# A branch prefetch hint on TensorE ahead of each expert's overflow branch

## The chip, the cores and the metric

The kernel runs on one core of a Trainium2 chip. The metric is device time in microseconds (us) of one execution. A core has five engines that each follow their own instruction stream: TensorE (PE; its weight loads are listed as PEld), VectorE (DVE), ScalarE (ACT), GpSimd (POOL) and SyncE (SP, which here issues the weight loads). Each engine has a sequencer that takes instructions in order, waits, branches and hands work to the engine; a "q" behind an engine's name in the trace (PEq, PEldq) is that sequencer.

## The reference

One layer of a hybrid block for 256 latent and 256 context tokens of width 1024, float32 throughout. Modulated RMSNorm, one input projection, four parallel token mixers (grouped attention, neighbourhood attention, Fourier, convolution), a gated merge, an output projection and a gated residual; then a second modulated RMSNorm and a mixture of 16 experts, of which each token uses two; a last RMSNorm. What matters here is the mixture:

```
gate = sum(one_hot(top_idx) * w)                    # two experts of each token
for e in range(16):
    a, b = split(t @ w_gu[e], 2)                    # 256 x 1024 @ 1024 x 1024
    out = out + gate[:, e] * ((silu(a) * b) @ w_down[e])
x = x + g2 * out
```

How many tokens an expert gets is known only when the router has run.

## The kernel before, in words

The first part (up to about 425 us of the span) computes the mixers and the router. The second part is a Python loop over the 16 experts, unrolled into one straight program. Each expert has room for 64 tokens (CAP) in its first block. Its tokens are gathered by one-hot products (`gather_step`, tiles `gag`), four experts at a time; `up` is the first product (tile `gue`, eight steps of two matmuls over the channels), `turned_hidden` turns its result (`hte`), `down` is the second product (`ye`), `slot_gate` (`gse`), `turned` (`ote`) and `scatter` (`sce`) bring the rows back to their tokens. `up` takes a list `beside`: after step k of the first product TensorE does the small pieces of work of the neighbours that stand in `beside[k]`, among them `turn_hidden` of the expert before in step 3.

An expert with more than 64 tokens needs more blocks. The count of each expert is in `cnt`; `values_load` (L1050) puts it in a register of TensorE, VectorE and ScalarE, and `tc.If(rv > CAP)` (L1076) stands around `overflow`, which does the whole chain again for the next 64 tokens, with two more levels inside it (L1078, L1080). The three levels are emitted for each expert, so each expert has a long piece of TensorE code that most executions jump over. All of the expert loop's matmuls are recorded by one helper and so have line L808 (turns: L811); they keep the order in which the code issues them, but a scheduler chooses where the branch of an expert falls between them. In this run's data two of the 16 experts overflow, those of index 5 and 13.

Expert weights come as 1 MB loads from SP (`load_units`, six for an expert: four for the first product, two for the second) into a ring of 16 buffers, each as soon as its buffer is free.

Of the kernel before, what the change touches and what calls it, by code (L numbers as in the profile page):

```python
# [16 lines left out]
ET = mybir.EngineType  # L17
# [4 lines left out]
S = 256  # L22
# [9 lines left out]
CAP = 64  # L32
KC = 31
EPS = 1e-6
# [3 lines left out]
# columns of the packed table of small operands  # L38
# [13 lines left out]
def mixer_moe(ctx: ExitStack, tc: tile.TileContext, A, out, dbg=None):  # L52
    nc = tc.nc
# [32 lines left out]
    # ---------------------------------------------------------------- constants and small operands  # L86
# [17 lines left out]
    # the gate of the second residual, its halves swapped in the second tile  # L104
    G2 = [cp.tile([P, 512], F32, name=f"G2_{i}") for i in range(2)]

    def rstd_of(dst, ssum, n, cols):
        """dst = (ssum / n + EPS) ** -0.5"""
        G.tensor_scalar(dst, ssum, 1.0 / n, EPS, op0=ALU.mult, op1=ALU.add)  # L109
        G.tensor_tensor(dst, dst, mhalf[:, 0:1].to_broadcast([P, cols]) if cols > 2 else mhalf[:, :cols], op=ALU.pow)  # L110
# [8 lines left out]
    # what the branches alone need  # L119
# [11 lines left out]
    def t4(name, shape, dt=F32):  # L131
        """an area of up to 1152 words"""
        n = int(np.prod(shape[1:]))
        t = bp.tile([P, 1152], dt, tag="t4", bufs=4, name=name)[:, :n]
        return t if len(shape) == 2 else t.rearrange("p (a b) -> p a b", a=shape[1])
# [9 lines left out]
    # ---------------------------------------------------------------- modulation  # L145
# [10 lines left out]
    def mod_set(s, out):  # L156
        """one third of the modulation, in steps; [p, j, b, r]: the value of column 512 j + 128 b + p, row r"""
# [19 lines left out]
    def mod_sums(i, res):  # L177
        """part i (of six) of the modulation, for the latent tokens only, without its bias: res gets [p, column],
        still to be summed over the partitions"""
# [16 lines left out]
    def mod_cols(i, dst):  # L196
        """the same as columns: dst [p, b] is its column 128 b + p"""
# [8 lines left out]
    # ---------------------------------------------------------------- norm1 of latent and context tokens  # L206
    def turned_norm(src, dst, xT, name):
        """src / rms, channels on the partitions"""
# [18 lines left out]
    def modulated(xT, r, name):  # L227
        """xT * a1 + sh1 in two parts"""
# [22 lines left out]
    # ---------------------------------------------------------------- streamed products, float32 in three passes  # L251
    aside = []
    n_prod = [0]
    # expert loads behind those of each of the last products
# [10 lines left out]
    def stream(src, kt, name, sub=V.tensor_tensor):  # L265
        """a chunk of 1 MB with kt rows per partition, as high and low part"""
# [12 lines left out]
    def product(src, kt, targets, name, ws=None):  # L279
        """targets: (psum, f) with f(k, w part, x part) -> (lhsT, rhs); w part and x part index (high, low)"""  # L280
# [18 lines left out]
    def in_cols(c0, name, kind, rs=(0,), ws=None):  # L299
        """256 columns of h @ w_in; one bank per token set: [tok, (t, col)] or [col, (ct, tok)]"""  # L300
# [11 lines left out]
    # rope tables with the gains folded in  # L312
# [10 lines left out]
    def rest_of_mod():  # L323
# [10 lines left out]
        # the gate of the second residual, its halves swapped in the second tile  # L334
# [16 lines left out]
    # ---------------------------------------------------------------- GQA projections  # L351
    def rope(dst, src, n, t, nh):
        """src [p, h, d] -> dst [p, h, d]"""
# [14 lines left out]
    def split(hi, lo, src, scale=None):  # L368
        """src = hi + lo, both exact in float32r"""
# [7 lines left out]
    def stacked(dst, lower, upper, eng):  # L377
        """dst [p, h, ..]: of the heads on the lower and the upper partitions, each head's part there stays, with
        that of the other operand beside it on the other half"""
# [11 lines left out]
    for t in range(NT):  # L391
# [5 lines left out]
        # heads (i, i + 4) side by side: the two key heads sit on the two halves of the partitions  # L397
# [37 lines left out]
    # ---------------------------------------------------------------- convolution branch, first part  # L435
# [15 lines left out]
    def conv_taps():  # L451
        for ct in range(CT):
# [5 lines left out]
            # z was kept without its factor 1/2  # L458
# [5 lines left out]
    # ---------------------------------------------------------------- attention  # L464
# [45 lines left out]
    # NA projections first, so that TensorE has work while the softmax of GQA runs  # L510
# [14 lines left out]
    def half(h, i):  # L525
        """all partitions for the first product of the scores, those of the head for the second"""
        return slice(64 * h, 64 * h + 64) if i else slice(0, P)
# [31 lines left out]
    # ---------------------------------------------------------------- Fourier branch  # L559
    def fourier():  # L560
# [5 lines left out]
        for g in range(4):  # L566
            # cosine and sine sums over the tokens, for the frequencies up to S / 2
# [10 lines left out]
            # the cosine part is even in the frequency, the sine part odd  # L578
# [37 lines left out]
    # ---------------------------------------------------------------- expert weights, in units of 1 MB  # L616
    # which buffers they take in turn
# [5 lines left out]
    def load_units(n):  # L623
        """the next n units: four of the first product's weights, two of the second's, for each expert"""
# [9 lines left out]
    # ---------------------------------------------------------------- gated merge of the branches  # L634
# [46 lines left out]
    # ---------------------------------------------------------------- output projection, residual, router logits  # L681
# [23 lines left out]
    # ---------------------------------------------------------------- routing  # L705
# [13 lines left out]
    # the scores of each group twice in a row, for sums of neighbours  # L719
# [15 lines left out]
    def rank4(v, n, name):  # L735
        """v [p, n, 4] -> how many of the four stand before each (larger, or equal with a lower index)"""
# [13 lines left out]
    # the sum of the two best of each group is the largest sum of two  # L750
# [14 lines left out]
    # 1-based place of each token in its experts' queues; 0 where not routed  # L765
# [13 lines left out]
    # the normalised rows in two parts, while TensorE counts  # L779
# [9 lines left out]
    # the table of the experts' activation, before it is waited for  # L789
# [9 lines left out]
    # ================================================================ mixture of experts  # L799
# [20 lines left out]
    def onehot(e0, ne, blk, name, tag, bufs):  # L820
        """[tok, expert, slot] for slots of block blk, per token tile"""
# [12 lines left out]
    def gather_step(hg, oh, k, name):  # L834
        """modulated rows of the tokens in the slots, for channel tile k, channels on the partitions"""
# [15 lines left out]
    def gather_one(oh, name):  # L851
        """the same for one block: rows first, then turned"""
# [21 lines left out]
    def slot_gate(oh, i, e, name, ov=False):  # L874
        """gate of the token in each slot, twice over the partitions"""
# [9 lines left out]
    def turned(e0, e1, blk, name, ov=False):  # L885
        """one-hots [slot, tok] of a block of two experts, one under the other"""
# [9 lines left out]
    def up(hg_of, gu, name, ov=False, beside=lambda k: None):  # L896
        """hidden of a block: half j of the columns sits on partitions 64 j .. 64 j + 63"""
# [20 lines left out]
    def down_raw(hT, dn, flip, name, ov=False):  # L918
        """output of a block: column half p ^ flip on partitions 64 p .. 64 p + 63"""
# [8 lines left out]
    def down(hT, dn, gsl, flip, name):  # L928
        """the same, gated, times the residual gate"""
# [45 lines left out]
    def finish(i):  # L975
        """second product of expert i's first block, its rows beside those of its pair, by column half"""
# [9 lines left out]
    def finish_last(i):  # L986
        """the same for the last expert, in column quarters and each scattered at once"""
# [29 lines left out]
    def turn_pair(pair, j):  # L1017
        """the pair one under the other, for the second column half in the other order"""
# [6 lines left out]
    def gate_of(i):  # L1025
        gates_[i] = slot_gate(ohs[i // 4], i % 4, i, f"e{i}")

# [19 lines left out]
    for i in range(NE):  # L1047
# [3 lines left out]
        # TensorE's smaller work of the neighbours, between the steps of the first product  # L1051
# [18 lines left out]
        q, hg = i % 4, hgs[i // 4]  # L1070
# [121 lines left out]
```

## Time and profile before

| | us |
|---|---|
| median of 3 runs | 772.96 |
| lowest, highest | 772.71, 775.69 |
| span of the profiled execution | 773.1 |

The profiled execution gives a span from its first to its last instruction, and no other time beside it. PE is busy 88% of it, DVE 55%, ACT 34%, POOL 9%. An instruction of a sequencer (a branch, a register load, a semaphore) does not count as busy; while one holds the sequencer, the engine works off what was handed to it earlier and then stands still. The chain of work that ended last is followed here only over the last few per cent, so the views to read are those of idle time on PE and of its branches.

### The profile page before, as it was taken

The page shows a single profiled execution, that of the slowest core. Times are in us where ns is not written, and L with a number is a line of the kernel's source. Part 1 is how long each engine was busy: PE and PEld are TensorE (multiplying, and loading weights), DVE is VectorE, ACT ScalarE, POOL GpSimd, SP SyncE. Part 2 cuts the span into 40 slices and gives each one's busy share as a digit, 9 for nine tenths or more (in the row PEclk, how much of TensorE's full clock was granted, in tenths as well). Part 3 has the DMA queues.
Part 4 walks back from the last instruction along what each step waited for, and adds up shares of the span by engine and source line. Part 5 has one row for each costly group of instructions (what it writes and reads, how often), then busy time and mean ns, then how long its engine had stood idle before and what let it go on. Part 6 is the DMA issues. An engine that isn't in the chain of part 4 may idle for free. (4 is left out here: it accounts for less than half of the span.)

```text
span 773.1 us, 11216 instructions
## 1 busy us (share of the span) xinstructions
PE 680.8 (88%) x4409; PEld 458.4 (59%) x4409; DVE 427.6 (55%) x844; ACT 261.5 (34%) x479; POOL 66.6 (9%) x94
## 2 busy tenths in 40 slices
PE   2689899999999999999997879899679879988784
PEld 0288899878878989999996323333224223422322
DVE  0379799888877965777564404332323323332335
ACT  1257755377565433435454101101111001101112
POOL 1124100113020012021110000000000000000001
PEclk9879999999999999999998889999899989999797
DMA  9885561635337876868855477893394998893301
GB/s 369 316 277 171 181 201 56 218 110 158 111 109 252 286 271 192 301 227 286 313 197 221 173 271 269 310 411 133 125 408 179 410 408 345 306 408 145 111 25 61
DMA packets 75132, 180.16 MB, mean 233 GB/s; under 512 B 3104, under 2 KB 39072, under 8 KB 74016
## 3 DMA queue, kind: packets, MB, share of 16 engines
q1 hardware_dynamic: 73088, 172.90, 61.7%
q0 software_dynamic: 1104, 3.15, 1.4%
q10 hardware_dynamic: 848, 2.85, 0.9%
q8 instruction: 63, 1.03, 0.6%
q14 instruction: 29, 0.24, 0.1%
HBM read 177.83 MB, written 1.05 MB: 231 GB/s over the span
## 5 line engine op out<-in xcount | busy, mean ns | idle before, releaser
L808 PE MATMUL gue<-we,hgg 128*64 128x512 f32 x512 | 145.4, 658 | 28.1 <-PEq L1076 20.3
L808 PEld LDWEIGHTS gue<-we,hgg 128*64 128x64 f32 x512 | 36.5, 147 | 72.8 <-issue 59.6
L287 PE MATMUL gl<-hhil,wh_gl 128*128 128x256 f32 x256 | 73.3, 287 | 0.0
L287 PE MATMUL gl<-hhil,wl_gl 128*128 128x256 f32 x256 | 72.8, 286 | 0.2
L287 PE MATMUL gl<-hlol,wh_gl 128*128 128x256 f32 x256 | 72.3, 283 | 0.0
L808 PE MATMUL ye<-we,hTe 128*64 128x512 f32 x256 | 65.4, 623 | 6.2 <-PEq L1078 3.6
L455 DVE SCALAR_TENSOR_TENSOR cv<-zp,pk,cv 128x256 f32<-128x256 f32 x120 | 51.3, 480 | 0.2
L906 ACT ACTIVATE sie<-gue 128x256 f32<-128x256 f32 x16 | 6.2, 384 | 127.9 <-PE gue L808 127.9
L287 PEld LDWEIGHTS gl<-hhil,wl_gl 128*128 128x128 f32 x256 | 48.0, 188 | 2.4 <-DVE wl_gl L275 1.9
L274 ACT CAST wh_gl<-w_gl 128x1024 fp32r<-128x1024 f32 x32 | 33.1, 1049 | 48.0 <-PE gl L287 24.0
L287 PEld LDWEIGHTS gl<-hhil,wh_gl 128*128 128x128 f32 x256 | 48.2, 188 | 1.5 <-issue 1.5
L287 PEld LDWEIGHTS gl<-hlol,wh_gl 128*128 128x128 f32 x256 | 48.3, 189 | 0.5 <-issue 0.5
L287 PE MATMUL z<-y,wh_br 128*128 128x256 f32 x256 | 47.2, 283 | 0.0
L808 PEld LDWEIGHTS ye<-we,hTe 128*64 128x64 f32 x256 | 19.7, 143 | 45.4 <-issue 44.3
L275 DVE TENSOR_TENSOR wl_gl<-w_gl,wh_gl 128x1024 fp32r<-128x1024 f32 x32 | 41.0, 1294 | 9.6 <-ACT wh_gl L274 9.5
L191 DVE SCALAR_TENSOR_TENSOR acc<-wv,csil,acc 128x512 f32<-128x512 f32 x56 | 41.1, 762 | 4.9 <-DMA wv<-in_w_mod_dram 4.9
L371 ACT CAST yh<-yse 64x512 fp32r<-64x512 f32 x30 | 18.5, 616 | 73.7 <-DVE yse L932 63.6
L287 PEld LDWEIGHTS z<-y,wh_br 128*128 128x128 f32 x256 | 39.4, 188 | 0.9 <-issue 0.7
L287 PE MATMUL z<-y,wl_br 128*128 128x256 f32 x128 | 36.7, 289 | 1.7 <-DVE wl_br L275 1.6
L932 DVE SCALAR_TENSOR_TENSOR yse<-ye,gsle,G 128x512 f32<-128x512 f32 x15 | 11.3, 750 | 41.5 <-PE ye L808 41.5
L940 DVE TENSOR_TENSOR xs<-xs,sce 128x512 f32<-128x512 f32 x28 | 19.2, 686 | 19.5 <-PE sce L808 19.5
L1097 POOL TENSOR_TENSOR fr<-fss 128x1 f32<-128x1 f32 x2 | 0.6, 280 | 340.1 <-ACT last L1095 340.1
(397 smaller groups left out, 1553.6 us busy)
## 6 DMA issues: line engine op xcount, KB each, us to landing
we<-in_w_gu_dram SPq DMA_DIRECT2D x64, 1024.0 KB, 8.7
we<-in_w_down_dram SPq DMA_DIRECT2D x32, 1024.0 KB, 9.2
wv<-in_w_mod_dram SPq DMA_DIRECT2D x16, 1024.0 KB, 5.3
w_gl<-in_w_in_dram SPq DMA_DIRECT2D x16, 1024.0 KB, 5.5
wm<-in_w_mod_dram SPq DMA_DIRECT2D x8, 1024.0 KB, 9.4
w_br<-in_w_branch_dram SPq DMA_DIRECT2D x8, 1024.0 KB, 5.1
w_out<-in_w_out_dram SPq DMA_DIRECT2D x4, 1024.0 KB, 7.3
w_gq<-in_w_in_dram SPq DMA_DIRECT2D x2, 1024.0 KB, 8.2
```

The source lines that it names most:

```text
L191: V.scalar_tensor_tensor(acc[:, s], wm[:, k % 2, s], csil[:, k, 0:1], acc[:, s], op0=ALU.mult, op1=ALU.add)
L274: SC.copy(w[0], raw[:, s])
L275: sub(w[1], raw[:, s], w[0].bitcast(F32), op=ALU.subtract)
L287: PE.matmul(dst, a, b, start=(k == 0 and wi + xi == 0), stop=(k == kt - 1 and wi == 1))
L371: SC.copy(hi, src)
L455: V.scalar_tensor_tensor(cv[:, ct, :], zp[:, ct, j : j + S], convw[:, ct, j : j + 1], cv[:, ct, :], op0=ALU.mult, op1=ALU.add)
L808: pinned(PE.matmul(*a, **k))
L906: SC.activation(si, acc[:, :256], AF.Silu)
L932: V.scalar_tensor_tensor(ys, y, gsl, G2[flip], op0=ALU.mult, op1=ALU.mult)
L940: V.tensor_tensor(ao, ao, o, op=ALU.add)
L1097: G.tensor_tensor(fr[:, 0:1], fss[:, t, 0:1], fss[:, t, 1:2], op=ALU.add)
```

## The change

In each expert's first product a function `hint` is called beside step 4. It marks a place for a prefetch hint, on TensorE alone, for the branch with label `ov{i}`, and keeps the instructions of the hint behind the TensorE instruction traced last. The branch of L1076 gets that label. The hint takes the condition `rv > CAP` as a register value: an ALU instruction on the register of the count, then the hint, which names the branch. All other lines of the diff drop comments.

```
+    def hint(i, rv):
+
+        traced = nc.cur_bb.bb.instructions
+        n, before = len(traced), next(x for x in reversed(traced) if x.engine == ET.PE)
+        tc.mark_branch_hint_location(f"ov{i}", rv > CAP, engines=[ET.PE])
+        for x in nc.cur_bb.bb.instructions[n:]:
+            assert x.engine == ET.PE
+            tc.add_manual_dep(x, before.name, mybir.DependencyInfo(mybir.DependencyClass.NoSync, mybir.DependencyReason.DATA),
+                              reason="hint")
...
         q, hg = i % 4, hgs[i // 4]
+        beside[4].append(lambda: hint(i, rv))
         hids[i] = up(lambda k: hg[k // 4][:, k % 4, CAP * q : CAP * q + CAP], W[i][0], f"e{i}",
...
-        with tc.If(rv > CAP):
+        with tc.If(rv > CAP, label=f"ov{i}"):
             overflow(i, 1, oh1)
```

What the built program holds: 12 pairs of an ALU instruction and a hint, for experts 3 and 5 to 15. For experts 0, 1, 2 and 4 the branch stands ahead of step 4 of that expert's first product, and no hint is there. Hint and branch are 46 to 77 TensorE instructions apart (a float32 matmul counts as two weight loads and two matmuls). On PE, around expert 9, before (the second product `ye8` is that of the expert before):

```order
L808 MATMUL gue9_8730<-we9_2_8277,hgg84_7862 64x512 x2
L808 MATMUL sce310_8763<-yh6_7919,oTe3_0_8325 128x512
L808 MATMUL sce310_8763<-yl6_7920,oTe3_0_8325 128x512
L808 MATMUL gue9_8730<-we9_3_8279,hgg84_7862 64x512 x4
L808 MATMUL sce311_8771<-yh6_7919,oTe3_1_8336 128x512
L808 MATMUL sce311_8771<-yl6_7920,oTe3_1_8336 128x512
L808 MATMUL ye8_8778<-we8_4_7790,hTe8_8753 64x512 x4
L808 MATMUL ye8_8778<-we8_5_7792,hTe8_8753 64x512 x4
L1076 COMPARE_AND_BRANCH
```

and now:

```order
L1032 REGISTER_ALU
L1199 BRANCH_PREFETCH_HINT
L808 MATMUL gue9_8757<-we9_2_8301,hgg84_7883 64x512 x2
L808 MATMUL sce310_8793<-yh6_7943,oTe3_0_8349 128x512
L808 MATMUL sce310_8793<-yl6_7944,oTe3_0_8349 128x512
L808 MATMUL gue9_8757<-we9_3_8303,hgg84_7883 64x512 x4
L808 MATMUL sce311_8801<-yh6_7943,oTe3_1_8363 128x512
L808 MATMUL sce311_8801<-yl6_7944,oTe3_1_8363 128x512
L808 MATMUL ye8_8808<-we8_4_7811,hTe8_8780 64x512 x4
L808 MATMUL ye8_8808<-we8_5_7813,hTe8_8780 64x512 x4
L1087 COMPARE_AND_BRANCH
```

The matmuls and the branch keep their places; two instructions are new. The same holds for experts 3, 5 to 8 and 10 to 15. Two branches move. That of expert 1, on PE before:

```order
L808 MATMUL gue0_4710<-we0_2_3305,hgg04_4742 64x512 x2
L808 MATMUL gag07_4773<-ohg00_4671,xh_4614 128x256
L808 MATMUL gag07_4773<-ohg00_4671,xl_4615 128x256
L808 MATMUL gag07_4773<-ohg01_4673,xh_4614 128x256
L808 MATMUL gag07_4773<-ohg01_4673,xl_4615 128x256
L808 MATMUL gue0_4710<-we0_3_3519,hgg04_4742 64x512 x4
L1050 TENSOR_LOAD cnt_4649
L1076 COMPARE_AND_BRANCH
```

and now:

```order
L808 MATMUL gag06_4763<-ohg01_4673,xh_4614 128x256
L808 MATMUL gag06_4763<-ohg01_4673,xl_4615 128x256
L808 MATMUL gue0_4710<-we0_2_3305,hgg04_4742 64x512
L1060 TENSOR_LOAD cnt_4649
L1087 COMPARE_AND_BRANCH
```

It stood behind the whole first product of expert 0, and stands now inside it, nine matmuls earlier. That of expert 2, on PE before:

```order
L808 MATMUL gue1_5158<-we1_1_4500,hgg00_4675 64x512 x4
L811 MATMUL hte0_5174<-pk_67,sie0_4783 128x128 x2
L808 MATMUL gue1_5158<-we1_2_4582,hgg04_4742 64x512 x4
L808 MATMUL gue1_5158<-we1_3_4657,hgg04_4742 64x512 x4
L808 MATMUL ye0_5190<-we0_4_4120,hTe0_5177 64x512 x4
L808 MATMUL ye0_5190<-we0_5_4245,hTe0_5177 64x512 x4
L1050 TENSOR_LOAD cnt_4649
L1076 COMPARE_AND_BRANCH
```

and now:

```order
L808 MATMUL gue1_5161<-we1_1_4500,hgg00_4675 64x512 x4
L811 MATMUL hte0_5177<-pk_67,sie0_4786 128x128 x2
L808 MATMUL gue1_5161<-we1_2_4582,hgg04_4742 64x512 x2
L1060 TENSOR_LOAD cnt_4649
L1087 COMPARE_AND_BRANCH
```

It moves from behind the second product of expert 0 into the first product of expert 1, 14 matmuls earlier.

## Rows read from the trace of the kernel before

**Rows 1.** The page, second part: the clock that TensorE was granted, by slices of 19.3 us
```profile
PEclk9879999999999999999998889999899989999797
```
**Rows 2.** Waits of PE: who waited for whom: us in total, times, longest
```profile
PE gue L808 <- PEq L1076: 20.3, 9, 5.6
...
PE ye L808 <- PEq L1076: 2.6, 3, 1.4
...
PE hte L811 <- issue: 2.5, 1, 2.5
...
PE gse L808 <- issue: 2.1, 1, 2.1
```
**Rows 3.** Line L1076 alone: engine op xcount: ns min/median/max, first and last start
```profile
L1076 PEldq COMPARE_BRANCH  x16: 82/3777/6452, 432.4 to 747.5; - x16
...
L1076 PEldq EVENT_SEMAPHORE  x14: 51/51/51, 435.8 to 751.3; - x14
```
**Rows 4.** Stretches from branch to restart, experts 3, 6 to 12, 14, 15
```profile
core 0: us, PE busy (x) PEld busy (x) DVE busy (x) ACT busy (x) POOL busy (x), PEclk, DMA share, GB/s
491.20:495.00 3.80, 2.40 (x12) 1.00 (x10) 1.14 (x3) 0.95 (x2) 0.00 (x0) 1.00 0.37 142
566.10:573.90 7.80, 3.04 (x16) 0.73 (x12) 2.65 (x6) 1.27 (x3) 0.00 (x0) 1.00 1.03 406
589.90:593.80 3.90, 3.22 (x14) 1.24 (x13) 1.11 (x2) 0.95 (x2) 0.00 (x0) 1.00 0.02 6
603.40:610.10 6.70, 4.47 (x26) 1.31 (x23) 1.80 (x4) 1.62 (x3) 0.00 (x0) 1.00 1.03 410
622.70:629.10 6.40, 3.58 (x16) 0.99 (x16) 1.69 (x4) 1.23 (x2) 0.00 (x0) 0.95 1.03 406
641.60:646.40 4.80, 4.49 (x28) 1.32 (x24) 1.24 (x3) 0.39 (x1) 0.00 (x0) 1.00 0.53 156
660.80:664.50 3.70, 3.19 (x14) 1.25 (x13) 1.11 (x2) 0.95 (x2) 0.00 (x0) 1.00 0.25 95
674.10:680.90 6.80, 4.47 (x28) 1.34 (x23) 1.83 (x5) 1.61 (x3) 0.00 (x0) 1.00 1.02 409
731.80:736.60 4.80, 4.49 (x28) 1.35 (x23) 1.22 (x3) 0.38 (x1) 0.00 (x0) 1.00 0.03 7
747.50:751.40 3.90, 3.60 (x17) 1.03 (x17) 1.09 (x3) 0.00 (x0) 0.00 (x0) 1.00 0.03 6
sum 52.60, PE 36.95 PEld 11.56 DVE 14.87 ACT 9.35 POOL 0.00; mean PE 3.69 PEld 1.16 DVE 1.49 ACT 0.94 POOL 0.00
```
**Rows 5.** The same for the six jumps without a hint; expert 1, and the sum
```profile
442.10:448.50 6.40, 0.80 (x6) 0.03 (x2) 0.39 (x2) 0.38 (x1) 0.00 (x0) 0.93 1.01 371
...
sum 31.10, PE 12.32 PEld 4.82 DVE 9.84 ACT 2.56 POOL 0.00; mean PE 2.05 PEld 0.80 DVE 1.64 ACT 0.43 POOL 0.00
```
**Rows 6.** The page, third part: DMA queue of the instructions, packets, MB, share
```profile
q8 instruction: 63, 1.03, 0.6%
```
**Rows 7.** DMA queues from 603.4 to 607.3 us, the one queue listed
```profile
q1 hardware_dynamic: 422, 1.60, 102.4%
```
**Rows 8.** DMA queues from 641.6 to 643.7 us, and then from 609.9 to 622.6 us
```profile
q8 instruction: 1, 0.02, 4.0%
...
q8 instruction: 1, 0.02, 0.5%
```
**Rows 9.** Stretches at a lower clock: one of five, the sum of five; the experts' part
```profile
573.90:577.30 3.40, 3.37 (x10) 1.55 (x12) 0.37 (x2) 0.00 (x0) 0.00 (x0) 0.50 1.04 410
...
sum 16.40, PE 16.20 PEld 6.08 DVE 4.37 ACT 0.00 POOL 0.00; mean PE 3.24 PEld 1.22 DVE 0.87 ACT 0.00 POOL 0.00
425.00:752.00 327.00, 281.77 (x1339) 107.03 (x1340) 107.12 (x242) 39.09 (x77) 0.46 (x1) 0.93 0.68 261
```
**Rows 10.** Order of time on PE, 434 to 470 us: eight matmuls twice
```profile
440.94 1.94 PE L808 MATMUL gue<-we,hgg 128*64 128x512 f32 x8
448.47 3.68 PE L808 MATMUL gue<-we,hgg 128*64 128x512 f32 x8 [5.60 <-PEq L1076]
```
**Rows 11.** Line L1078 from 553 to 554 us: a jump over a few instructions
```profile
L1078 PEldq COMPARE_BRANCH  x1: 193/193/193, 553.1 to 553.1; - x1
```

## Prediction

> **What bounds the kernel now.** I read the page first, then the waits of PE, then the branch line by itself, then stretches of time around each branch. PE is the engine that sets the pace of the experts' part: from 425 to 752 us it is busy 281.77 of 327.00 us, DVE 107.12, ACT 39.09, and the data queues are in use 0.68 of the time [rows 9]. So 45 us are idle on PE, and the waits say what ended them: 20.3 us in front of the first product and 2.6 us in front of the second are put down to PE's own sequencer at L1076, the overflow branch [rows 2]. No other engine is late there; the sequencer itself had no instruction to give.
>
> The branch line alone shows the price. It has 16 records on PE from 82 to 6452 ns with a median of 3777 ns, and 14 of them are followed by the semaphore that only the not-overflowing arm holds [rows 3]. So 14 branches jump over an overflow block and take microseconds, while two fall through into it, at 82 ns. A jump over a few instructions takes 193 ns [rows 11]. So it is not the jump that is dear but that its target is far. Instructions come by a queue of their own, 63 packets of together 1.03 MB, so 16 KB each [rows 6]. In the stretch after the branch at 603.4 us that queue has no packet for 3.9 us, while the weight queue holds 102.4% of the DMA engines [rows 7]; after that at 641.6 us, with less weight traffic, its packet comes within 2.1 us [rows 8]. I read this as: a far jump waits for the fetch of its target, about 3.7 us when the DMA engines are free and about 6.3 us when weights are loading. The stretches agree: those with a DMA share over 1 last 6.4 to 7.8 us until PE restarts, those with one of 0.02 to 0.53 last 3.7 to 4.8 [rows 4].
>
> PE does not stand for the whole of this, since it works off what it was handed: 2.40 to 4.49 us of each stretch are busy [rows 4].
>
> **The change part by part.** *Hints that can pay.* Twelve branches get a hint. Experts 5 and 13 overflow, so theirs fall through and have nothing to gain. Ten remain. Their stretches sum to 52.60 us with 36.95 us of PE work in them, so 15.65 us are idle [rows 4]. If the target is there when the branch comes, the branch costs about 0.19 us [rows 11], under at least 2.40 us of queued work, and PE sees none of it. Gain 15.65 us, bounds 0 and 15.65.
>
> Is it there in time? Eight matmuls with their eight weight loads take 1.94 us [rows 10], 0.12 us an instruction, and the hints of those ten stand 62 to 77 instructions ahead: an estimate of 7.5 to 9.3 us at PE's pace, against a fetch of up to 6.5 us [rows 3]. If it is a microsecond late, the queued work still covers it.
>
> *Second stalls.* Two idle times with the releaser "issue", 2.1 us in front of `gse` and 2.5 us in front of `hte` [rows 2], are of the same family: they come a few matmuls after a landing (experts 9 and 15), where the code runs out of the block that was fetched and the next one is still under way. 24 new instructions shift every later landing within its 16 KB block. By counting instructions, expert 15 now lands just behind a border and not just ahead of it, so its 2.5 us should go; expert 9 still lands ahead of one, but with queued work left I expect half of the 2.1 to stay. Gain 3.6 us, bounds -2.5 (a new one elsewhere) and 4.6. Here the Trainium skill, Runtime: NRT & Kernel Launch, section Instruction fetch mechanics, says that crossing such a border costs a queue bump that is mostly hidden. By that the term would be 0 and the time 3.6 us later; the two waits, one of 2.1 and one of 2.5 us, differ from it just behind a jump.
>
> *The clock.* Five stretches of together 16.40 us run at the lower of the two clock levels, 1.2 instead of 2.4 GHz, each behind one of these stalls; PE is busy 16.20 us of them [rows 9]. Eight matmuls take 3.68 us there against 1.94 [rows 10], so about 8.2 us are lost. Without the idle time ahead of them I expect most, not all, to go, as the page shows dips in other places too [rows 1]: gain 6 us, bounds 0 and 8.2.
>
> *What is added.* 24 sequencer instructions. The trace has no row for either kind; the nearest are the semaphore at 51 ns [rows 3] and the near jump at 193 ns [rows 11], so 1.2 to 4.6 us of the sequencer's time in all. Each pair falls where PE has queued work (2.40 us or more), which hides it. I take 0; bounds 0 and 4.6, the latter if they came when the queue is empty.
>
> *What moves.* The branches of experts 1 and 2 stand 9 and 14 matmuls earlier and have no hint. The six jumps without a hint (these, experts 0 and 4, and two inner ones of experts 5 and 13) hold 31.10 - 12.32 = 18.78 us of idle, which stays. Expert 1's stretch has 0.80 us of work in 6.40 [rows 5]: there is hardly any cover to lose. Behind the moved branches now wait the rest of the first product and the ACT and DVE steps that follow it, which earlier ran during the stall. I take 0, bounds -1.3 and 1.3.
>
> *What is late next.* Weights: the only DMA wait charged to expert weights ends with expert 6's branch, and a share of 0.68 over 327 us [rows 9] becomes 0.74 over 302. PE stays the bound.
>
> Sum: 15.65 + 3.6 + 6 = 25.2 us. The profiled execution has a span of 773.1 us and no other time beside it, the median of the runs is 772.96, so they are the same within 0.2. 773.1 - 25.2 = 748 us.
>
> **Rivals.** *The hint does nothing.* All ten hints that could pay come when the code has long entered the 16 KB block in which the branch stands, and by then the fetcher has used its look-ahead: from the landing of expert 8 at 609.9 us to the branch of expert 9 at 622.6 there is just one instruction packet [rows 8]. If it looks ahead once for each block, a hint in the middle of it comes too late, and the 15.65 us stay. What remains is the shift of the landings: 773.1 - 2.5 + 1 = 771.5 us, between 769 and 776. The Trainium skill, same page and section, says that prefetch is purely sequential. By that rule no hint would matter, and it would be this rival; that far targets are missing in all 14 jumps agrees with it, but before the change no hint asked for one. Against it: the queue is idle between that packet and the branch, so nothing stands in the way of one more.
>
> *It helps in part.* The hinted fetch is late where weights load, or held back by the look-ahead of the block. Half of 15.65, of the clock term a third and the 2.5 of expert 15: 773.1 - 7.8 - 2 - 2.5 = 761 us.
>
> *The fetcher follows the wrong arm.* If the register's value is read the other way, the ten get nothing, and for experts 5 and 13 the target is fetched in place of the code that follows. These two then stall in the overflow block, each by a fetch of 3.7 to 6.4 us that the queued work covers in part, say 3 us, and the shift may set a new second stall of 2.5: 773.1 + 6 + 0 to 2.5, so 779 us. The case decides itself by the two records of 82 ns: they, or the idle time just behind them, would grow to microseconds. Nothing in the profile speaks for it; that the two experts run three nested pieces of code straight through is why it would be felt.
>
> **How the numbers follow.** The forecast has a chance of 0.63, part help 0.10, no effect 0.20, the wrong arm 0.07. 0.5% is 3.9 us, about what a measurement of this kernel tells from no change. Faster than 769.1: the forecast, part help, and a sliver of no effect, 0.75. Within 0.5%: 0.18. Slower: 0.07. The forecast's own range: 15.65 with 0 to 8.2 of clock and -2.5 to 4.6 of second stalls gives 745 to 760 at the ends; with late gains in both places 743. The range that holds 8 in 10 must take in part help and the lower half of no effect: 743 to 772.
>
> **What would show it.** Right: the branch records of experts 3, 6 to 12, 14 and 15 drop to about 0.2 us; each hint is followed by an instruction packet ahead of its branch; the idle time put down to L1076 falls from 22.9 us to about 12; expert 9's and 15's stretches keep the full clock. Experts 0, 1, 2 and 4 still show 3 to 6 us. Wrong: records of 3.7 and 6.3 us as before (no effect), or a packet in place but a stall behind the landing (part help), or microseconds at experts 5 and 13 (wrong arm). If the records drop and the time does not, PE was not the bound, and a wait for weights must have grown.

## The result and the profile after

The changed kernel takes 751.29 us (median of 4 runs, 748.82 to 755.24), the kernel before 774.23 us (4 runs, 772.71 to 775.69). The medians differ by 22.9 us. The ratio is 0.972, with an interval of 0.968 to 0.976: 2.8% faster. The forecast was 748 us with a range of 743 to 772. The profiled execution of the changed kernel is one of its longer ones, 755.2 us with a span of 753.5; it has to be read against the span of 773.1 before, so 19.6 us. One execution of all those in this document, 775.39 us of the run with old places and no fetch, was in a slower state and is left out of that run's numbers. In after, line numbers are eleven higher: the overflow branch is L1087, the inner one L1089.

The page of the kernel after, second and third part: the clock by slices of 18.8 us, and the queue of the instructions with packets, MB and share.

```profile
PEclk9879999999999999999999789999989999999897
...
q8 instruction: 61, 1.00, 0.5%
```

The dips in the middle of [rows 1] are fewer, and the number of packets is 61 against 63 [rows 6]: the hints do not add traffic, they bring the same blocks earlier.

Next the waits of PE in after (us in total, times, longest), which answer to [rows 2].

```profile
PE gue L808 <- PEq L1087: 15.2, 9, 5.4
...
PE ye L808 <- PEq L1089: 3.1, 1, 3.1
...
PE gue L808 <- DVE ohv L830: 1.8, 1, 1.8
...
PE ye L808 <- issue: 0.5, 1, 0.5
...
PE hte L811 <- PEq L1087: 0.2, 1, 0.2
```

Both second stalls, 2.1 us ahead of `gse` and 2.5 us ahead of `hte`, are gone. What the overflow branch holds up has fallen from 20.3 + 2.6 to about 15.7 us (two smaller rows with it). The branch line and the new instructions, as in [rows 3]:

```profile
L1087 PEldq COMPARE_BRANCH  x16: 80/1782/6867, 434.7 to 731.5; - x16
...
L1199 PEldq BRANCH_PREFETCH_HINT  x12: 30/38/46, 488.3 to 723.2; - x12
...
L1032 PEldq ALU_OP  x12: 37/37/51, 488.2 to 723.1; - x12
```

The median of the branch is 1.8 instead of 3.8 us; its maximum of 6.9 us is that of expert 1, which has no hint. The stretches behind the ten hinted branches, cut as in [rows 4] from the branch to the restart of TensorE (where it never stopped, to the branch's end), show what the hints did. The rows are those of experts 3, 6, 8, 12 and 15, and the sum of all ten.

```profile
core 0: us, PE busy (x) PEld busy (x) DVE busy (x) ACT busy (x) POOL busy (x), PEclk, DMA share, GB/s
494.50:494.90 0.40, 0.40 (x4) 0.26 (x3) 0.00 (x0) 0.14 (x1) 0.00 (x0) 1.00 1.06 420
568.70:573.50 4.80, 3.04 (x16) 0.76 (x13) 1.81 (x5) 0.94 (x3) 0.00 (x0) 1.00 1.00 391
...
600.90:605.70 4.80, 4.49 (x28) 1.35 (x23) 1.20 (x3) 0.38 (x1) 0.00 (x0) 1.00 1.03 411
...
659.80:666.20 6.40, 4.41 (x25) 1.27 (x21) 1.82 (x5) 1.51 (x3) 0.00 (x0) 1.00 1.02 405
...
731.50:731.80 0.30, 0.30 (x3) 0.13 (x4) 0.30 (x2) 0.00 (x0) 0.00 (x0) 1.00 0.00 0
sum 31.50, PE 26.44 PEld 8.46 DVE 8.86 ACT 4.30 POOL 0.00; mean PE 2.64 PEld 0.85 DVE 0.89 ACT 0.43 POOL 0.00
```

Idle of TensorE in the ten: 31.50 - 26.44 = 5.1 us, against 15.65 before. Expert 3's branch is cured (0.4 us in place of 3.8). Expert 8's record is still 2.7 us long, but queued work covers all but 0.3. Expert 6's record is 1.8 us long and ends 3.0 us ahead of the restart, so that its 1.8 us of idle time have another reason (see the earlier hint below). Expert 12's is not helped at all: 6.4 us, 2.0 of them idle.

That one branch shows how a hint is missed. Its hint comes at 656.2 us. The DMA queues from 656.3 to 663.2 us, and then from 663.2 to 665.9 us (the two queues of interest):

```profile
q1 hardware_dynamic: 725, 2.79, 101.5%
q8 instruction: 1, 0.02, 1.0%
...
q1 hardware_dynamic: 273, 1.05, 98.3%
q8 instruction: 1, 0.02, 2.6%
```

The branch itself begins at 659.8 and takes 6114 ns:

```profile
L1087 PEldq COMPARE_BRANCH  x1: 6114/6114/6114, 659.8 to 659.8; - x1
```

I read the first packet, 0.7 us behind the hint, as the fetcher's ordinary look-ahead: the kernel before has such a packet without any hint, 2.5 us ahead of expert 12's branch (here 2.8). The block asked for is then the second, at 663.3 us, and the branch ends 1.5 us after it has landed. With idle DMA engines, expert 15's hint is answered at once. From this hint at 723.2 us to its branch at 731.5 the only packet of any queue stands in the sixth of 40 slices, 1.0 to 1.2 us behind the hint:

```profile
GB/s 0 0 0 0 0 80 0 0 0 0 0 0 0 0 0 0 0 0 0 0 0 0 0 0 0 0 0 0 0 0 0 0 0 0 0 0 0 0 0 0
```

The experts' part as a whole, from its first `gue` to its last `ye`, in before and then in after:

```profile
427.70:760.30 332.60, 285.61 (x1357) 107.20 (x1356) 107.40 (x238) 40.31 (x78) 0.00 (x0) 0.93 0.66 256
```

```profile
429.30:740.30 311.00, 278.65 (x1357) 105.33 (x1356) 108.01 (x238) 40.27 (x78) 0.00 (x0) 0.95 0.71 274
```

It is 21.6 us shorter: TensorE is idle 46.99 us before and 32.35 after (14.6 less), and busy 285.6 and 278.7 us with the same 1357 matmul records (7.0 less). The busy time falls because less of it runs at the lower clock. All stretches at half clock inside that part, summed in before (nine) and then in after (four); it also begins in one, 2.9 us of it before and 4.4 after:

```profile
sum 44.20, PE 36.08 PEld 14.68 DVE 10.41 ACT 0.00 POOL 0.00; mean PE 4.01 PEld 1.63 DVE 1.16 ACT 0.00 POOL 0.00
```

```profile
sum 23.80, PE 17.69 PEld 6.75 DVE 4.35 ACT 0.56 POOL 0.00; mean PE 4.42 PEld 1.69 DVE 1.09 ACT 0.14 POOL 0.00
```

So 20.4 us less in these, and 18.9 with the one at the start. All five stretches of [rows 9] are gone. The four that are left stand at the jumps of experts 1 and 4 and the inner ones of 5 and 13, which have no hint.

### The profile page after: what moved, and what is told of

Read it like the earlier page. It is cut to its first block, busy times and chain, and to the rows that moved or that the text cites. A ratio compares the mean times of both kernels' runs of the same rounds, so it can differ in the third digit from the quotient of the medians.

```text
span 753.5 us, 11239 instructions
## 1 busy us (share of the span) xinstructions
PE 674.2 (89%) x4409; PEld 456.6 (61%) x4409; DVE 427.2 (57%) x844; ACT 261.5 (35%) x479; POOL 66.5 (9%) x94
## 5 line engine op out<-in xcount | busy, mean ns | idle before, releaser
L808 PE MATMUL gue<-we,hgg 128*64 128x512 f32 x512 | 141.2, 634 | 19.9 <-PEq L1087 15.2
L808 PEld LDWEIGHTS ye<-we,hTe 128*64 128x64 f32 x256 | 19.6, 140 | 42.4 <-issue 41.3
L666 POOL TENSOR_TENSOR merged<-merged,gt 128x512 f32<-128x512 f32 x12 | 19.4, 1616 | 117.1 <-DVE gt L665 117.1
L808 PEld LDWEIGHTS gag<-ohg,xh 128*128 128x128 f32 x64 | 13.0, 204 | 27.4 <-issue 13.5
```

What stands on the lines that cost most here:

```text
L666: G.tensor_tensor(mt, mt, gts[c], op=ALU.add)
L808: pinned(PE.matmul(*a, **k))
```

## Experiments

**The hint's sense.** The first run asks for the other arm; everything stands in the same place.

```
-        tc.mark_branch_hint_location(f"ov{i}", rv > CAP, engines=[ET.PE])
+        tc.mark_branch_hint_location(f"ov{i}", rv <= CAP, engines=[ET.PE])
```

> The hint's register holds the opposite condition (count at most 64 in place of over 64); every instruction stands where it stands in the changed kernel. Theory (the gain is the fetch that the hint asks for): the ten hinted branches that jump hold TensorE's sequencer for 3.3 to 6.5 us again, each as in the kernel before; half-clock stretches and the idle time behind L1076 come back, time 769 to 775 us. Rival 1 (the gain is the shift of the landings by 24 instructions and the two moved branches): 750 to 755 us as with the hint. Rival 2 (a hint for the wrong arm takes the place of the look-ahead in the code that follows): experts 5 and 13, which are now told to expect the jump and fall through, stall just behind the branch by 2 to 5 us each, time 775 to 782 us; the theory without this rival has no idle time there.

Measured 765.03 us, ratio 0.985 (0.981 to 0.989): the theory's stalls, but 4 us below its range, as the shift of the landings is worth more than I had counted (next run) and two inner jumps have become short. The outer branches are back at microseconds, and the two that fall through stay near 0.1 us, with no idle time behind them: a wrong guess costs those two nothing. Lines L1087 and L1089:

```profile
L1087 PEldq COMPARE_BRANCH  x16: 91/4290/6711, 433.5 to 741.8; - x16
...
L1089 PEldq COMPARE_BRANCH  x4: 193/270/364, 550.6 to 716.0; - x4
```

The second row was not expected: the far inner jumps of experts 5 and 13 take 0.36 us, though no hint names them. In the next run, where no hint acts, the same jumps take 3.7 and 3.4 us, and from the outer branch's hint to the inner jump there is one instruction packet less for each of the two. By the count of instructions the packet that expert 5's wrong hint brought at 522.4 us holds the code that its inner jump goes to, and I read the row as that block still being there 28 us later.

**No fetch at all.** A hint whose condition is never true leaves all the added instructions and every moved branch.

```
-        tc.mark_branch_hint_location(f"ov{i}", rv > CAP, engines=[ET.PE])
+        tc.mark_branch_hint_location(f"ov{i}", rv < 300, engines=[ET.PE])
-        rv = nc.values_load(..., min_val=0, max_val=S)
+        rv = nc.values_load(..., min_val=0, max_val=4 * S)
```

> The hint's register always holds the value for no jump (count below 300, which it always is); instructions and their places as in the changed kernel. Theory: no hinted fetch, the ten branches at 3.3 to 6.5 us, 769 to 774 us; the difference to the run with the other sense is the price of two wrong hints. Rival 1 (landings and moved branches): 750 to 755 us. Against the kernel before this also prices the 24 added instructions and the shift by themselves: the 2.5 us in front of expert 15's turn should be gone, the 2.1 us behind expert 9's landing still there.

Measured 766.92 us, ratio 0.991 (0.988 to 0.994) to 775.02 us of the kernel before beside it, so 8.1 us faster with no hint that acts, and 2 us below the theory's range. Its experts' part:

```profile
425.90:752.50 326.60, 281.97 (x1357) 106.68 (x1356) 107.48 (x238) 40.27 (x78) 0.00 (x0) 0.95 0.67 261
```

6.0 us shorter than before: 2.4 idle and 3.6 busy. From here to the changed kernel it is 15.6 us more: 12.3 idle and 3.3 busy. That is what the fetches themselves are worth. The second stall ahead of `hte` is gone here too. So is the one behind expert 9, against expectation; a new one ahead of `gse` has come behind expert 10's landing:

```profile
PE gse L808 <- issue: 1.8, 1, 1.8
```

**An earlier hint.** The hint goes beside step 1 of the product instead of step 4, so 82 to 130 instructions ahead of its branch. Expert 0 gets a hint too, 0.5 us ahead of its branch and so too late.

```
-        beside[4].append(lambda: hint(i, rv))
+        beside[1].append(lambda: hint(i, rv))
```

> The hint beside step 1 of the first product in place of step 4, so 82 to 130 instructions ahead of its branch and not 46 to 77. Theory A (the hinted fetch was late where weights load): the records that were still 1.8 to 2.7 us for experts 6, 8, 10 and 14, and 6.1 us for expert 12, fall to 0.5 us or less; time 3 to 5 us below the changed kernel, 746 to 749 us. Rival B (only one fetch can be under way, and a hint that meets the block's own look-ahead is lost): the early hints of experts 9, 10, 11 and 12, which come just behind a landing or a border while weights load, do nothing; their records go back to 5.7 to 6.5 us and the time is 752 to 760 us. If such a hint is only put off, records of 0.5 to 3 us.

Measured 748.74 us, ratio 0.966 (0.963 to 0.969). Line L1087:

```profile
L1087 PEldq COMPARE_BRANCH  x16: 80/370/6337, 432.2 to 725.0; - x16
```

The median falls to 0.37 us, and expert 12's record from 6.1 to 0.42. So hints are put off, not dropped, and at step 4 they came too late. Two records miss the theory's 0.5 us: expert 10's with 0.95 and expert 14's with 2.0. Expert 14's hint comes at 700.7 us together with a look-ahead packet and gets its own packet only at 708.7 us, though by the count of instructions it stands in its branch's block and the DMA engines are idle at the end of that wait; in the run with all hints below the same wait is 7.7 us. What puts it off that long these runs do not show.

Shorter records did not make all ten stretches free of idle time. Expert 6's, and the sum of the ten cut as above:

```profile
563.50:568.30 4.80, 3.06 (x18) 0.79 (x13) 1.83 (x5) 0.94 (x3) 0.00 (x0) 1.00 1.03 407
...
sum 29.30, PE 26.09 PEld 7.88 DVE 8.02 ACT 2.78 POOL 0.00; mean PE 2.61 PEld 0.79 DVE 0.80 ACT 0.28 POOL 0.00
```

So 3.2 us are left of 5.1. What ends them are instructions behind the branch. First expert 8, whose branch record is 0.33 us; then the loads of counts behind expert 6's branch:

```profile
L1087 PEldq COMPARE_BRANCH  x1: 334/334/334, 595.7 to 595.7; - x1
...
L1087 PEldq EVENT_SEMAPHORE  x1: 51/51/51, 600.2 to 600.2; - x1
...
L1060 PEldq TENSOR_LOAD <-cnt x2: 299/304/308, 566.8 to 567.5; - x2
```

The semaphore that only the not-overflowing arm holds comes 4.2 us behind the branch, 0.06 us after the last matmul handed out ahead of it has ended (600.12 us), and the next matmul starts at 600.43. I read it as a wait for these matmuls: 0.3 us of idle time, however short the jump. At expert 6 two loads of counts with their checks stand behind it, 1.7 us in all. The waits list puts that down to VectorE's `ohv`, but the sequencer's own records fill it.

Expert 3 shows a put-off of another kind. Its hint now stands in the 16 KB block ahead of the one that holds its branch. From that hint to 486.4 us, the queues:

```profile
DMA packets 792, 3.05 MB, mean 398 GB/s; under 512 B 48, under 2 KB 48, under 8 KB 792
## 3 DMA queue, kind: packets, MB, share of 16 engines
q1 hardware_dynamic: 792, 3.05, 101.5%
```

No instruction packet for 7.7 us. It comes, by the count of instructions, when the code enters the branch's own block; expert 3's record is 0.37 us all the same.

**The inner jumps as well.** Inside an overflow block a second hint stands behind its gather, for the inner branch.

```
     def overflow(e, blk, oh, inner=lambda: None):
 ...
         hg = gather_one(oh, n)
+        inner()
 ...
-            overflow(i, 1, oh1)
-            with tc.If(rv > 2 * CAP):
+            overflow(i, 1, oh1, lambda: hint(i, rv, 2))
+            with tc.If(rv > 2 * CAP, label=f"ow{i}"):
```

> In addition a hint inside the overflow block, behind its gather, for the inner branch (second overflow block). Two executions of it, in experts 5 and 13. Theory: the two inner branches fall from 3.3 and 3.5 us to under 0.5, the 3.05 and 2.97 us of idle TensorE behind them shrink to below 1 us, and part of the half-clock stretches of 6.8 us behind them goes: 6 to 10 us below the changed kernel, 741 to 746 us. Rival (the work behind them waits for the last additions of the overflow block on VectorE, not for instructions): idle time of the same size with another releaser, 749 to 753 us. Experts 0, 1, 2 and 4 get a hint one instruction ahead of the branch here, which should change nothing for them: 3.3 to 6.9 us.

Measured 752.48 us, ratio 0.972 (0.969 to 0.975): no better than the change, and far from the theory's 741 to 746. Expert 5's inner jump falls to 0.38 us, expert 13's does not:

```profile
L1090 PEldq COMPARE_BRANCH  x4: 197/292/3836, 550.3 to 704.3; - x4
```

Counting instructions to 16 KB blocks explains both sides. Expert 13's inner branch now stands 13 instructions behind a border and its hint ahead of that border; the same befell the outer branches of experts 6 and 7, 6 and 8 instructions behind one, whose records are 5.99 and 3.33 us again. If a hint acts only in its branch's block, it has no time there. By these records the one inner jump gained 3 us and these two lost 4 and 3.

**The change again, and the branches that moved.** In the second run here, experts 0, 1, 2 and 4 get no hint in the source, so that the branches of experts 1 and 2 keep their old places; the third does the same with a condition that is never true.

```
-        beside[4].append(lambda: hint(i, rv))
+        if i not in (0, 1, 2, 4):
+            beside[4].append(lambda: hint(i, rv))
```

> The changed kernel once more, beside the three that follow, to have all four on one scale. Both theories: 751 us (749 to 755), a ratio of 0.97 to the kernel before; the branch records of experts 6, 8, 10 and 14 between 1.5 and 3 us and that of expert 12 near 6 us as in its first profile, if the lateness lies in the program's positions and not in chance.

> Hints for experts 3 and 5 to 15 only, and none written for 0, 1, 2 and 4; so the branches of experts 1 and 2 stay in their old places, while the 24 added instructions and the twelve hints are those of the change. Theory S (what the change gains beyond the fetches comes from the shift of the later landings): 751 us, as the changed kernel. Theory M (it comes from the branches of experts 1 and 2 that stand earlier): 3 to 7 us longer than the changed kernel, 754 to 758.

> As the run before it, with a hint that is never taken (a value below 300 is asked for, and there is always one), so only the 24 instructions are left of the change, and no branch moves. Theory S: 767 us, as the run with moved branches and hints never taken (ratio 0.991), the wait of 2.5 us ahead of expert 15's turn gone. Theory M: 772 to 774 us, a ratio of 0.997 to 1.000, although the 2.5 us are gone.

Measured, beside 774.31 us of the kernel before: the change again 751.57 us, ratio 0.970 (0.967 to 0.974); old places 750.72 us, ratio 0.970 (0.967 to 0.973); old places and no fetch 766.5 us, ratio 0.989 (0.986 to 0.992). The moved branches are worth nothing that can be measured, and theory M falls. The shift of the landings alone gains 7.8 us. In the change's second profile the records of experts 6, 8, 10 and 14 are 2.5, 2.8, 2.3 and 1.8 us and expert 12's is 6.1 again, as expected: the lateness belongs to the places in the program. Expert 12's also hangs on a little time: in the run with old places no packet comes between its hint and the one for its target, and the record is 2.6 us.

**The last landing alone.** Only experts 13, 14 and 15 get a hint, one that is never taken: six instructions.

```
-        tc.mark_branch_hint_location(f"ov{i}", rv > CAP, engines=[ET.PE])
+        tc.mark_branch_hint_location(f"ov{i}", rv < 300, engines=[ET.PE])
 ...
-        beside[4].append(lambda: hint(i, rv))
+        if i in (13, 14, 15):
+            beside[4].append(lambda: hint(i, rv))
```

> The kernel before with six sequencer instructions only: a hint that is never taken for experts 13, 14 and 15. By counting instructions only the last landing changes its place against a 16 KB border, from 4 instructions ahead of one to 2 behind it. Theory P (what the 24 instructions gain without a fetch is expert 15's second stall and the half-clock stretch behind it): the 2.5 us wait ahead of hte and the stretch near 755 us go, others stay; 2.5 + 1.7 = 4.2 us, 770 us, ratio 0.9945, half or more of the 7.4 us. Theory Q (the gain is spread over the landings of experts 9 to 12 as well): 0 to 2.5 us, 772 to 774 us, ratio 0.997 to 1.000.

Measured 769.46 us, ratio 0.9946 (0.992 to 0.997), 4.2 us with an interval of 2.3 to 6.0: theory P's number, while the 0 to 2.5 us of theory Q touch only the interval's edge. Waits of PE:

```profile
PE gse L808 <- issue: 3.5, 1, 3.5
...
PE hte L811 <- PEq L1088: 0.2, 1, 0.2
```

The wait ahead of `hte` has gone from 2.5 to 0.2 us, and the 3.4 us behind the landing run at the full clock, where before had a half-clock stretch from 754.8 to 758.2:

```profile
749.90:753.30 3.40, 2.55 (x20) 1.22 (x20) 2.80 (x6) 1.23 (x2) 0.00 (x0) 1.00 0.49 149
```

The second stall behind expert 9, whose landing did not move, is still there (3.5 us in this profile, 2.1 in before).

**All the hints that can work.** Beside step 1 for the ten; right behind the load of the count for expert 0 (55 instructions ahead) and expert 4 (14); behind the gather in the overflow blocks of experts 5 and 13, whose outer branches lose theirs.

```
         rv = nc.values_load(cnt[0:1, i : i + 1], ...)
+        if i in (0, 1, 2, 4):
+            hint(i, rv)
 ...
-        beside[4].append(lambda: hint(i, rv))
+        if i not in (0, 1, 2, 4, 5, 13):
+            beside[1].append(lambda: hint(i, rv))
 ...
+            overflow(i, 1, oh1, (lambda: hint(i, rv, 2)) if i in (5, 13) else lambda: None)
```

> Hints where the experiments so far say that they work: beside step 1 for the ten experts that can gain, 55 instructions ahead for expert 0, 14 ahead for expert 4, and in the overflow blocks of experts 5 and 13 117 instructions ahead of the inner branch, in its own 16 KB block; none for the outer branches of 5 and 13. Theory A (a hint in its branch's block at least some 6 us ahead takes the whole stall; what is left is what has no hint or a late one): records of experts 0, 5 inner and 13 inner 0.3 to 1 us, idle in the experts' part down by 1.6 + 2.6 + 2.5, and 742 to 745 us, ratio 0.957 to 0.961. Rival B (the fetches take turns with the weights and with the look-aheads, so that more hints move the stalls elsewhere): 748 to 751 us, as with the hints beside step 1 alone.

Measured 741.36 us (740.07 to 744.37), ratio 0.958 (0.955 to 0.961): the best version, 33 us faster than before and 10 than the change. The page's clock row, then the waits of PE, then the two branch lines:

```profile
PEclk9979999999999999999999889999999999999998
```

```profile
PE gue L808 <- PEq L1091: 10.0, 8, 3.8
...
PE gue L808 <- DVE ohv L830: 1.7, 1, 1.7
...
PE ye L808 <- PEq L1093: 0.5, 1, 0.5
```

```profile
L1091 PEldq COMPARE_BRANCH  x16: 75/364/6121, 430.3 to 716.6; - x16
...
L1093 PEldq COMPARE_BRANCH  x4: 200/286/446, 544.3 to 691.8; - x4
```

All inner jumps are under 0.45 us, and expert 0's is 0.49. Experts 1 and 2 have no hint in the instruction stream, as their branches are placed ahead of it; expert 4's, 0.3 us ahead of its branch, is too late by far. These three hold 3.8 + 1.8 + 2.9 = 8.5 of the 10.0 us. Theory A's 742 to 745 is just missed on the good side.

**A floor.** The last run has no overflow block, no branch and no one-hot of a second block for the 14 experts that do not need them, and no hint.

```
-        beside[4].append(lambda: hint(i, rv))
 ...
+        if i not in (5, 13):
+            continue
         oh1 = onehot(i, 1, 1, f"v{i}_1", "ohv", 1)
         with tc.If(rv > CAP, label=f"ov{i}"):
```

> Leaves out the overflow blocks, their branches and the one-hot of the second block for the 14 experts that do not overflow; experts 5 and 13 keep theirs, without hints. So it is a floor for what hints can do, not a kernel for other inputs. From the run with all useful hints (741.4 us): theory A (what is left there is the unhinted jumps of experts 1, 2 and 4, 3.8 + 1.8 + 2.9 us with some 2 us of clock, and small register waits) gives 741.4 - 10.5 + 5.5 for the two inner jumps that are unhinted here = 736 us, 733 to 739. Rival B (TensorE would be late for weights once the jumps are gone): 741 us or more, with DMA waits ahead of gue in the place of the jumps.

Measured 720.17 us, ratio 0.931 (0.928 to 0.933): 16 us below theory A's number, a miss. Rival B, TensorE late for weights, fails by more. The experts' part of the best version and then of this one:

```profile
426.50:725.40 298.90, 277.23 (x1357) 104.07 (x1356) 107.92 (x238) 40.32 (x78) 0.00 (x0) 0.97 0.74 285
```

```profile
426.60:703.70 277.10, 268.06 (x1357) 101.46 (x1356) 103.06 (x210) 40.28 (x78) 0.00 (x0) 0.98 0.78 306
```

The idle time is 21.7 and 9.0 us: 12.6 less, of which 8.5 are the three unhinted jumps, 1.7 the loads of counts behind expert 6's branch, and the rest small waits behind the other branches. That was expected in kind. The other 9.2 us are busy time for the same matmuls, and little of it is clock (0.97 and 0.98). Without the branches the order of the work on TensorE is another one, and I did not separate that. So hints take back 33 of 53 us; a share of the rest is not the fetch.

The inner jumps are short here though nothing hints at them:

```profile
L1091 PEldq COMPARE_BRANCH  x4: 181/260/363, 527.8 to 670.3; - x4
```

By the count of instructions they cross only one border in this program, from block 27 to 28 and from 34 to 35, and the block after the one that runs had been fetched by the look-ahead (one packet 7.2 us ahead of the first of them). In the other programs they jump over a whole block, and take 3.3 to 3.8 us.

## Why the prediction was right

*Hinted jumps, 15.65 us forecast.* 10.6 measured (15.65 - 5.1), the step that was most off. The mechanism is the one named, a fetch of the target before the branch. Two things in the step failed. One is "Is it there in time?": from hint to branch I had estimated 7.5 to 9.3 us, and it was 6.2 to 8.2 in five of the ten and 3.6 to 4.9 for experts 6, 8, 10, 12 and 14. I had timed it by the matmuls, and the sequencer, which handles hint and branch, runs ahead of them: it reaches the branch with 2.4 to 4.5 us of matmuls still to run [rows 4]. And the price of a hinted fetch was set at that of an unhinted one, with no wait for the look-ahead. This cost 1.9 us, nearly all at expert 12: with the hint beside step 1 the ten stretches hold 3.2 us in place of 5.1. The other is "PE sees none of it": these 3.2 us stay behind records of 0.33 to 0.95 us (expert 14: 2.0), as the semaphore and the loads of counts behind the branch still hold TensorE. [rows 4] had shown it: behind two fetches that queued work covers, 4.80 us hold 4.49 us of work. All of the experts' part has 4.0 us less idle time with the earlier hint (28.35 us against 32.35); the rest of that is mainly expert 1's jump, which has no hint and holds TensorE for 1.9 us less in that execution.

*Second stalls, 3.6 forecast.* 4.1 measured: 2.1 + 2.5 in before, 0.5 in after. Expert 15's went as the count of instructions said, and with six instructions alone. Expert 9's half did not stay: its stall is gone with the shift alone, where a new one of 1.8 us has come behind expert 10's landing, and that one went with the fetch. The Trainium skill, Runtime: NRT & Kernel Launch, section Instruction fetch mechanics, calls the crossing of a border mostly hidden; right behind a landing these runs show up to 3.5 us, and the measurement decides.

*The clock, 6 forecast.* 7.0 us less busy time, 18.9 us less at the lower level. Right in size, but half of it (3.6 us) comes with the shift of the landings and not with the fetch.

*Added instructions and moved branches, 0 and 0.* 24 records of 37 and 38 ns are 0.9 us on the sequencer, in a program that with them and no fetch is 7.8 us faster; moving the two branches changed nothing (751.57 and 750.72 us).

*The sum.* 10.6 + 4.1 of idle and 7.0 of clock are 21.7, which is the 21.6 us of the experts' part; 25.2 had been forecast. The profile's 19.6 us is smaller by 2.0 that lie outside of that part, which starts 1.6 us later in this execution. That the sum came so close is in part luck. The fetch gave 15.6 us (12.3 idle, 3.3 busy), where 15.65 and most of the clock's 6 had been counted on; the shift gave 6 to 8, where 3.6 had.

*The rivals.* "The hint does nothing" was wrong, and so is its rule from the same section of the Trainium skill, that prefetch is purely sequential: 1.2 us behind a hint a packet comes with no branch in sight, and the branch then takes 0.35 us. But this rival's time was mis-sized too. It gave 771.5 us to a program with the shift alone, and 767 is what that takes, from 774 to 775 of the kernel before beside it: I had counted the 2.5 us of expert 15 and a loss of 1, and left out the half-clock stretch behind that wait (1.7 us) and some 3 us more, whose place among the other landings the runs do not settle. "Helps in part" was half true, in its mechanism and not in its size. "The wrong arm" could be tried, and costs the two fall-through experts nothing.

*The signs.* The idle time of the branch fell to 15.7 and not 12; five of ten records fell under 0.8 us (0.35 at best, not 0.2), four to 1.8 to 2.7, one not at all; for experts 8 and 12 the packet comes behind the start of the branch and not ahead of it; experts 9 and 15 keep the full clock; experts 0, 1, 2 and 4 show 3.4 to 6.9 us, about as said.

## What to carry to other kernels

A far jump on TensorE costs the fetch of its target, 3.3 us with free DMA engines and up to 6.9 under load; ScalarE and VectorE take the same branches in 40 to 72 ns. A hint some 100 instructions ahead brought the branch under 0.5 us in eight of ten jumps here; one that came together with a look-ahead was put off by 8 us. By the count of instructions, it should stand in the same 16 KB block as the branch. Count the sequencer's time to the branch, not the matmuls'. What stands behind the branch, a semaphore or register loads, keeps its own price (0.3 and 1.7 us here) however fast the jump. The two jumps into the very next block needed no hint. And any edit that adds instructions moves all later landings against the borders: try the edit with its effect switched off before the gain is put down to the effect, since here a third of it (7 to 8 of 23 us) was the shift.

## What the runs showed of the hardware

- A hint costs 38 ns, and its fetch 1.2 us to the packet with idle DMA engines, 3.5 to 5.2 us with weights loading (eight hints of the change, DMA share 0.66 to 1.04).
- A hint that meets a look-ahead can be put off: 7.1 us from hint to packet for expert 12, 8.0 for expert 14 with the hint beside step 1, where the look-ahead had landed 6.7 us earlier. By the count of instructions, a hint in an earlier block waits for the block of its branch (7.7 us).
- The semaphore behind a jump comes 0.06 us after the last matmul ahead of it ended, 4.2 us behind a branch of 0.33 us (expert 8, hint beside step 1).
- TensorE's fetcher keeps a block for a while: one brought by the wrong hint at 522.4 us served, as I read it, a jump at 550.6 us, with one other packet between. The Trainium skill, Runtime: NRT & Kernel Launch, section Instruction fetch mechanics, speaks of a window of two pages outside of which a taken branch must fetch. The jump into the next block agrees with it. Here, by the count of instructions, the running block, the one after it and the hinted one were held together, and the measurement decides.
- A jump that falls through takes 80 ns, a short one 0.19 us, one to a block that is there 0.35 us.
